# A residual kept by features, or by tokens with a turn at each joint

## The chip, the core and the metric

The kernel runs on one core of a Trainium2 chip. Five engines run their own instruction streams: TensorE (PE) multiplies matrices out of SBUF into PSUM, VectorE (DVE) and ScalarE (ACT) do elementwise work on either memory, GpSimd (POOL) does little here beyond starting DMAs that add into SBUF, and SyncE (SP) starts the other DMAs. The metric is the device time of one execution in microseconds (us).

A matmul has a stationary operand of 128 x 128, loaded into the array before it, and a moving operand that streams past it, here up to 512 columns. In the rows of the profile the moving operand is named first: `ps<-actH,wh` streams `actH` past the stationary `wh`.

## The reference

One layer of a streaming encoder on 512 tokens with 1024 features:

```
h = h + 1/2 * SwiGLU_1(RMSNorm(h))             # 1024 -> 2 x 2816 -> 1024
z = RMSNorm(h) @ W_in                          # conv value, gate, q, k, v, r, low-rank gate
h = h + concat([conv module, gated linear attention]) @ W_out
h = h + 1/2 * SwiGLU_2(RMSNorm(h))
h = h + sigmoid(RMSNorm(h) @ W_g) * (p @ W_p)
out = RMSNorm(h)
```

Everything is float32. A contraction over features needs both operands with features on the partitions; a sum over the features of one token (the RMSNorm) and the output are by tokens.

## The kernel before

**Numbers.** Each float32 operand of a large product is split into two parts that the fast matmul format holds: a high one (a copy on ACT, `act.copy` or `AF.Copy` with a scale) and a low one (source minus high, on DVE). A product is three matmuls: high x high, high x low, low x high (`mm3`, `mul`, `part`). For some weights the subtraction is done by a DMA of POOL that adds into SBUF (`added`): ACT writes the high part and the negated source.

**Layout of the residual.** The residual stream is eight tiles `hT[0..7]` of 128 features x 512 tokens. x arrives by tokens, is turned on PE by 128 x 128 transposes (`turn_x`), and copied into `hT` (`keep_x`, line 461). The down projection of a SwiGLU (`second`, line 745) and the output projection (`part`, line 1228) have the weight as the stationary side, so their PSUM results have features on the partitions and are added to `hT` by DVE. The last stage needs tokens on the partitions, so `inputs` (line 1571) turns pieces of `hT` back, four transposes a call, eight calls.

**RMSNorm.** The gain of the next norm is applied when the high and low parts `hgH`, `hgL` are made. The factor of each token is applied to the results of the product instead, as a row spread over the partitions (`rsb`). `Norm` squares every `hT` tile on ACT, adds the squares on DVE, and sums over partitions with four matmuls against ones (`colsum`).

**Up projections.** Most pairs of column blocks use a scheme of seven products of half-sized blocks (`m1` to `m7`, class `Left` for weight sums, class `Right` for sums of activations). `Right.pieces` makes scaled copies `xg` of `hT` on ACT, and `sums1`, `sums2` add and subtract them on DVE. The last stage (gate with `W_g`) uses the same scheme with tokens as rows (`row_sums`, `row_diff`, `row_last`).

**Down projection.** The 22 blocks of hidden features are cut in five (`CUTS`): four of four blocks, one of six. A cut is four pieces; a piece (`piece`) makes two blocks of 128 output features, from one weight tile of four blocks x 256 columns; each block ends with one DVE add into `hT`. The last cut is done in two halves of three blocks. Pieces stand between the units of the next pair; in the steady state a pair is `m6 m7 m5 m1 m2 piece m4 m3 piece`. Before each unit `drive` issues what later units need: weight loads on SP seven or nine units ahead, the split of a weight four units ahead. Loaded weights, their high and their low parts have six buffers each (`raw`, `wh`, `wl`).

**Order.** From the start to line 1669 the instructions of PE, DVE and ACT each stay in the order in which they are written (`Ordered`). Behind that line the compiler orders them by readiness. PSUM has seven banks for products (`bank`) and one more (`aux`).

**Joints.** Three places take the residual to the next normed product: from the first SwiGLU to `W_in` (line 934), from `W_out` to the second SwiGLU (lines 1356 to 1438), and from the second SwiGLU to the last stage (line 1678). At each, `hgH` of a block is made by ACT directly behind its add, and `hgL` by DVE.

Of the kernel before, what the change touches and what calls it, by code (L numbers as in the profile page):

```python
# [15 lines left out]
P = 128  # L16
# [16 lines left out]
CUTS = ((0, 4), (4, 8), (8, 12), (12, 16), (16, 22))  # L33
# [29 lines left out]
def block_kernel(ctx: ExitStack, tc: tile.TileContext, a: dict, out: bass.AP):  # L63
# [169 lines left out]
    def zblock(w, x, mid={}):  # L233

        ps = bank()
        for k in range(DC):
# [49 lines left out]
    class Norm:  # L286
        def __init__(self, engine=dve):
            self.engine = engine
            self.acc = bt(s="sqacc")
            self.n = 0  # L290

        def add(self, h):
            if self.n == 0:
                act.activation(self.acc, h, AF.Square)
            else:
                sq = tmp("sq", bufs=3)
                act.activation(sq, h, AF.Square)
                self.engine.tensor_tensor(out=self.acc, in0=self.acc, in1=sq, op=ALU.add)
            self.n += 1

        def rows(self):
            return rsqrt_mean(colsum([self.acc]), D, TB)

# [25 lines left out]
    class Right:  # L329
# [3 lines left out]
        def __init__(self, rows, gname):  # L333
            self.rows, self.gname = rows, gname
            self.raw, self.op = {}, {}
            for k in range(2):
                for half in range(2):
                    hs = slice(half * HALF, (half + 1) * HALF)
                    self.op[f"b{k + 1}{half + 1}"] = [tuple(t[:, hs] for t in rows[4 * k + c]) for c in range(4)]

        def pieces(self, k, jp):

            for half in range(2):
                t = self.raw[k, half, jp] = two(bt(s="xg"))
                for jj in range(2):
                    c = 4 * k + 2 * jp + jj
                    act.activation(t[:, jj], hT[c][:, half * HALF:(half + 1) * HALF], AF.Copy, scale=vec(self.gname, c))
# [29 lines left out]
        def steps(self):  # L377

            def go(*todo):
                return lambda *_: [f() for f in todo]  # L380

            return [go(lambda: self.pieces(0, 0)),
                    go(lambda: self.pieces(1, 0), lambda: self.sums1(0)),
                    go(lambda: self.pieces(0, 1), lambda: self.sums2(0)),
                    go(lambda: self.pieces(1, 1), lambda: self.sums1(1)),
                    go(lambda: self.sums2(1))]
# [51 lines left out]
    hT = [big.tile([P, SEQ], F32, tag="H", bufs=DC, name=nm("h")) for _ in range(DC)]  # L438
    hg, xps, xt, squares = [], [], {}, []

    def load_x(c, n):

        nt = TB // n
        for h in range(n):
            tile_ = bt(s="x").rearrange("p (t c) -> p t c", t=nt)
# [14 lines left out]

    def keep_x(c):
        (act.copy if c % 2 else dve.tensor_copy)(hT[c], xps[c])
# [87 lines left out]
    xb = Right(hg, "ffn1_norm")  # L550
    steps = xb.steps()
    steps[0]()
    steps[1]()
# [50 lines left out]
    def ffn(w_in, w_out, x, gname, given, first, rsb, hooks, plain):  # L604


        norm = Norm()
        nhg = []
# [19 lines left out]
        def plus(ps, t, i, name):  # L628
            o = tmp(name)
            dve.tensor_tensor(out=o, in0=ps, in1=t, op=ALU.add)  # L630
            dve.tensor_tensor(out=two(o), in0=two(o), in1=row(i), op=ALU.mult)
            return o
# [31 lines left out]
        def m2(p):  # L664
# [3 lines left out]
            def gate0():  # L668
                p.s0 = silu(plus(p.y, p.a, 0, "g1"))
# [11 lines left out]
        def m5(p):  # L681
            mul(p.x, p.part("s1"), x.op["t1"], False, False)
            p.u = plus(p.w, snap(p.x, "sq", bufs=3), 1, "u1")

        def m4(p):
            mul(p.w, p.part("a22"), x.op["t4"], False, True)
            gated(p, p.s0, plus(p.w, p.u2, 0, "u1"), 0)
# [6 lines left out]
        def plain_unit(j):  # L694

            up, i, k = j // 4, j // 2 % 2, j % 2
            def run(p):
# [15 lines left out]
                return [lambda: gated_block(p, p.s[i], scaled(ps, "u1"), i),  # L713
# [31 lines left out]
        def second(cut):  # L745

            f0, f1 = cut
            last = f1 == CUTS[-1][1]
            kn = f1 - f0
            nk = kn // 2 if last else kn  # L750
            ps = {}

            def piece(n, g, begin, final, key=None):

                def get():
                    got[f0, n, g] = load(w_out, f0 + g * nk, nk, n * P, 2 * P)

                def make():
                    got[f0, n, g] = parts(got[f0, n, g])

                def run():
                    left = []
                    wh, wl = got.pop((f0, n, g))
                    for i in range(2):
                        if begin:
                            ps[n + i] = bank()
                        cs = slice(i * P, (i + 1) * P)
                        for kk in range(nk):
                            k = g * nk + kk
                            f = f0 + k  # L770
                            mm3(ps[n + i], wh[:, kk, cs], wl[:, kk, cs], *pairs[f // 2].acts[f % 2],
                                k == 0, k == kn - 1)
                        if final:
                            h = hT[n + i]
                            dve.scalar_tensor_tensor(out=h, in0=ps[n + i], scalar=0.5, in1=h,
                                                     op0=ALU.mult, op1=ALU.add)
                            if last:
                                hi = bt(F32R, "hgH")
                                act.activation(hi, h, AF.Copy, scale=vec(gname, n + i))
                                left.append((h, hi, vec(gname, n + i)))  # L780
                    if key:
                        hooks.get(key, lambda *_: None)()
                    if not left:
                        return []

                    def lower():
                        for h, hi, g in left:
                            lo = bt(F32R, "hgL")
                            dve.scalar_tensor_tensor(out=lo, in0=h, scalar=g, in1=hi.bitcast(F32),
                                                     op0=ALU.mult, op1=ALU.subtract)  # L790
                            nhg.append((hi, lo))

                    lower()
                    for h, *_ in left:
                        norm.add(h)

                return [(7, get), (AHEAD, make)], run

            if not last:
                return [piece(n, 0, True, True, ("g2", f0) if n == 0 else None) for n in range(0, DC, 2)]  # L800
            return ([piece(n, 0, True, False, ("last", n)) for n in range(0, 6, 2)],
                    [piece(n, 1, False, True, ("rest", n)) for n in range(0, 6, 2)]
                    + [piece(6, 0, True, False, ("rest", 6)), piece(6, 1, False, True, ("rest", 7))])

# [19 lines left out]
        for i in range(start, npair):  # L824
# [3 lines left out]
            if i == end:  # L828
                half, rest = second(cut_of[i])
                units.append(half[0])  # L830
# [10 lines left out]
        units += half[1:] + rest  # L841
# [3 lines left out]
        def first_out(norm_of_rows):  # L845
            got["rsb"] = norm_of_rows
            for i in range(2):
                s = silu(scaled(first[i][0], "g1"))
                gated_block(p0, s, scaled(first[i][1], "u1"), i)
# [7 lines left out]
        return nhg, norm  # L857
# [4 lines left out]
    def sums_hooks(x, names, at):  # L862

        h = {}
        for name, key in zip(names, at):
# [4 lines left out]
    hooks.update({("h%d" % (i + 1), 1): f for i, f in enumerate(steps[2:])})  # L870
    hooks.update({("m5", 3): lambda *_: made[0](), ("m5", 4): lambda *_: constants(),
                  ("m4", 10): lambda *_: w_ahead.append(ahead(w_in, D_CONV, 2 * P)),
                  ("last", 4): lambda *_: w_ahead.append(ahead(w_in, 0, 2 * P))})
    hg, norm = ffn(ffn1_in, a["ffn1_w_out"][0], xb, "mix_norm", {0: Left(ffn1_in, 0), 1: w1},
                   (ps0[:2], ps0[2:]), lambda: spread(mid[0]), hooks, (1, 2))
# [65 lines left out]
    pb0 = zblock(wb[0], hg)  # L941
# [6 lines left out]
    pa0 = zblock(wa[0], hg, {1: lambda: mid.append(rsqrt_mean(colsum([norm.acc]), D, TB))})  # L948
# [267 lines left out]

    def oload(n):
        for i in range(n, n + 2):
            raw_o[i] = load(a["w_out"][0], 0, DC, i * P, P)

    def ohigh(n):
        return (high4 if n in (4, 5) else high)(raw_o[n])
# [5 lines left out]
    def part(ps, w, ks, first, last, mid={}):  # L1228
        for k in ks:
            if k in mid:  # L1230
                mid[k]()
            (wh, wl), (xh, xl) = rows_of(w, k), mix[k]
            pe.matmul(ps, wh, xh, start=(first and k == ks[0]), stop=False)
            pe.matmul(ps, wl, xh, start=False, stop=False)
            pe.matmul(ps, wh, xl, start=False, stop=(last and k == ks[-1]))

    def first_part(n, w, mid={}):
        ps = bank()
        part(ps, w, range(4, 8), True, False, mid)
        half[n] = (w, ps)  # L1240

    oload(0)
    wo, rt = {n: added(ohigh(n)) for n in (0, 1)}, []
    for t in range(TB):
# [20 lines left out]
        if t == 1:  # L1265
            oload(2)
            wo[4] = [added(w) for w in ohigh(4)]
# [7 lines left out]
        if t == 2:  # L1275
            wo[5] = [added(w) for w in ohigh(5)]
# [15 lines left out]
    wo[2] = added(ohigh(2))  # L1292
# [8 lines left out]
    first_part(0, wo[0])  # L1301
    first_part(1, wo[1])
# [6 lines left out]
    low(wo[3])  # L1309
# [476 lines left out]
```

## Time and profile before

| what | value |
|---|---|
| median of 3 runs | 947.41 us (947.36 to 948.08) |
| profiled execution | 947.17 us |
| its span, first to last instruction | 945.5 us |
| mean granted TensorE clock | 0.997 |
| busy PE, DVE, ACT, POOL | 934.8, 747.0, 471.6, 56.4 us |
| HBM read, written | 93.61, 2.10 MB |

Rows of instruction groups give busy time, the mean length of one in ns, and the idle time in front. Nearly all instructions pass through one helper, so every row has line L46; the tile names tell them apart. Matmuls overlap their neighbours: the length of one is more than the distance from one start to the next, and it is the distance that counts on the path.

### The profile page before, as it was taken

The numbers are of one execution on the slowest core, as the hardware profiler recorded it, in microseconds if no ns is written. First come the engines' busy times: TensorE is split into PE (matmuls) and PEld (weight loads), VectorE is DVE, ScalarE is ACT, GpSimd is POOL, SyncE is SP. The second block draws the span as 40 slices with busy tenths as digits, with TensorE's granted clock in tenths as the row PEclk, the third lists the DMA queues.
The fourth block names the chain that finished last, engine by engine and source line by source line (L and its number), as shares of the span: only waits on it lengthen the run. The fifth ranks groups of instructions, "written<-read, shape, count | busy, mean of one in ns | idle before, by whom it ended". The sixth has DMA issues, their size and how long they took to land.

```text
span 945.5 us, 14381 instructions
## 1 busy us (share of the span) xinstructions
PE 934.8 (99%) x5770; PEld 828.2 (88%) x5770; DVE 747.0 (79%) x1021; ACT 471.6 (50%) x713; POOL 56.4 (6%) x71
## 2 busy tenths in 40 slices
PE   9999999999999999999999999999999999999996
PEld 7888999999999988788877889999999999998885
DVE  6786887887788566999986749787878787866896
ACT  5752544334443574463564855444434433445882
POOL 0000200000000110001030010000000000000121
PEclk9999999999999999999999999999999999999998
DMA  7532223242223593346552571432243224347463
GB/s 229 182 123 74 94 79 119 94 134 89 91 89 112 146 254 84 77 109 161 134 132 74 151 178 45 134 110 70 89 134 112 68 91 132 97 149 222 90 111 112
DMA packets 107686, 112.88 MB, mean 119 GB/s; under 512 B 5139, under 2 KB 96453, under 8 KB 107620
## 3 DMA queue, kind: packets, MB, share of 16 engines
q1 hardware_dynamic: 101732, 94.67, 31.9%
q0 software_dynamic: 5872, 17.30, 10.3%
q8 instruction: 45, 0.74, 0.3%
q14 instruction: 21, 0.17, 0.1%
q10 hardware_dynamic: 16, 0.00, 0.0%
HBM read 93.61 MB, written 2.10 MB: 101 GB/s over the span
## 4 chain that ended last, share of the span: by engine, by line
PE 99%; DVE 0%; ACT 0%; POOLq 0%; issue 0%; POOL 0%
PE ps L46 97%; PE ax L46 1%; DVE y L46 0%; POOLq L1782 0%; ACT ycH L46 0%; DVE yc L46 0%; ACT hgH L46 0%; DVE rs L46 0%; ACT s L46 0%; DVE u L46 0%; DVE g L46 0%; DVE s L46 0%; POOL ident masks.py:199 0%; DVE ms L46 0%; POOL mean L46 0%
## 5 line engine op out<-in xcount | busy, mean ns | idle before, releaser
L46 PE MATMUL ps<-hgH,wh 128*128 128x256 f32 (+1 forms) x768 | 238.4, 315 | 0.3 <-ACT hgH L46 0.3
L46 PE MATMUL ps<-hgL,wh 128*128 128x256 f32 (+1 forms) x768 | 237.6, 314 | 0.0
L46 PE MATMUL ps<-hgH,wl 128*128 128x256 f32 (+1 forms) x768 | 237.3, 314 | 0.0
L46 DVE TENSOR_TENSOR wl<-wr,wh 128x1024 fp32r<-128x1024 f32 (+2 forms) x162 | 189.6, 1181 | 47.8 <-ACT wh L46 47.7
L46 ACT CAST wh<-wr 128x1024 fp32r<-128x1024 f32 (+2 forms) x176 | 176.7, 1019 | 30.8 <-PE ps L46 16.3
L46 PEld LDWEIGHTS ps<-hgH,wh 128*128 128x128 f32 x768 | 146.3, 191 | 11.2 <-issue 1.1
L46 PEld LDWEIGHTS ps<-hgL,wh 128*128 128x128 f32 x768 | 146.1, 191 | 9.2 <-issue 0.2
L46 PEld LDWEIGHTS ps<-hgH,wl 128*128 128x128 f32 x768 | 146.4, 191 | 8.8
L46 PE MATMUL ps<-actH,wh 128*128 128x512 f32 x352 | 137.4, 390 | 0.0
L46 PE MATMUL ps<-actL,wh 128*128 128x512 f32 x352 | 137.3, 390 | 0.0
L46 PE MATMUL ps<-actH,wl 128*128 128x512 f32 x352 | 136.9, 389 | 0.0
L46 ACT ACTIVATE s<-g 128x512 f32<-128x512 f32 x48 | 30.4, 633 | 194.3 <-DVE g L46 194.3
L46 DVE SCALAR_TENSOR_TENSOR cv<-glu,cw,cv 128x502 f32<-128x502 f32 (+24 forms) x120 | 81.0, 732 | 0.6
L46 PEld LDWEIGHTS ps<-actH,wl 128*128 128x128 f32 x352 | 66.1, 188 | 14.1
L46 PEld LDWEIGHTS ps<-actH,wh 128*128 128x128 f32 x352 | 66.2, 188 | 12.9
L46 PEld LDWEIGHTS ps<-actL,wh 128*128 128x128 f32 x352 | 66.2, 188 | 12.5
L46 DVE SCALAR_TENSOR_TENSOR h<-ps,h 128x512 f32<-128x512 f32 x80 | 54.1, 687 | 22.2 <-PE ps L46 22.0
L46 ACT COPY sq<-ps 128x512 f32<-128x512 f32 x38 | 22.1, 585 | 73.8 <-PE ps L46 73.8
L46 DVE TENSOR_TENSOR wl<-sm,wh 128x1024 fp32r<-128x1024 f32 x38 | 46.2, 1221 | 1.2 <-ACT wh L46 0.9
L46 ACT CAST actH<-m 128x512 fp32r<-128x512 f32 x44 | 25.5, 618 | 37.3 <-DVE m L46 37.2
L46 ACT CAST wh<-sm 128x1024 fp32r<-128x1024 f32 x38 | 39.5, 1043 | 5.5 <-DVE sm L46 2.9
L46 DVE TENSOR_TENSOR u<-ps,sq 128x512 f32<-128x512 f32 x17 | 11.7, 691 | 34.8 <-ACT sq L46 34.8
(267 smaller groups left out, 1729.5 us busy)
## 6 DMA issues: line engine op xcount, KB each, us to landing
wr<-in_ffn_w_in SPq DMA_DIRECT2D x84, 512.0 KB
wr<-in_ffn_w_out SPq DMA_DIRECT2D x32, 512.0 KB
wr<-in_w_in SPq DMA_DIRECT2D x20, 512.0 KB
wl<-wr POOLq DMA_DIRECT2D x15, 512.0 KB, 5.5
wr<-in_ffn_w_out SPq DMA_DIRECT2D x16, 384.0 KB
wr<-in_w_out SPq DMA_DIRECT2D x8, 512.0 KB
wq<-in_ple_w_gate SPq DMA_DIRECT2D x8, 512.0 KB
wl<-wq POOLq DMA_DIRECT2D x8, 512.0 KB, 5.1
```

The costliest lines, as they stand in the source:

```text
L46: inst = call(*args, **kwargs)
```

## The change

The residual is now one tile `hall` of 128 tokens x 4 x 1024 features, into which x is loaded. The down projection and the output projection have the activations (by 128 tokens) as the stationary side and 512 columns of weight as the moving side; the DVE add that puts the product into `hall` also applies half the norm's factor, which is now one number a partition (`rsh`), so three multiplications by the spread row are dropped from the gating. Squares for the next norm are summed along the row on ACT (`accum_out`), so `colsum` and the DVE adds of squares go. At each joint a new class `Turn` transposes `hall` back to features, eight chunks of four transposes, in two halves of four chunks; ACT and DVE split each chunk out of PSUM, and where the seven-product scheme follows, ACT also writes the two scaled copies (`keep`) that `pieces` wrote before. The transposes of `inputs` go, since the last stage reads `hall`.

The last cut is 20 to 22 now, behind one of 16 to 20. A piece is one half of the output columns and two blocks of tokens; its weight tiles serve two pieces. The tiles of `W_out` are two rows of blocks x 512 columns.

```diff
-CUTS = ((0, 4), (4, 8), (8, 12), (12, 16), (16, 22))
+CUTS = ((0, 4), (4, 8), (8, 12), (12, 16), (16, 20), (20, 22))
...
+        def keep(self, ps, c, by_dve=False):
+            k, jp, jj = c // 4, c % 4 // 2, c % 2
+            for half in range(2):
+                if not jj:
+                    self.raw[k, half, jp] = two(bt(s="xg"))
+                o, src, g = self.raw[k, half, jp][:, jj], ps[:, half * HALF:(half + 1) * HALF], vec(self.gname, c)
+                if by_dve:
+                    dve.tensor_scalar(o, src, g, None, ALU.mult)
+                else:
+                    act.activation(o, src, AF.Copy, scale=g)
...
+    class Turn:
+        def done(self, t, e):
+            act.activation(tmp("sq", bufs=3), h_of(t, e), AF.Square, accum_out=self.ss[:, e * TB + t:e * TB + t + 1])
+
+        def chunk(self, c):
+            ps = bank()
+            for t in range(TB):
+                pe.transpose(ps[:, t * P:(t + 1) * P], hall[:, t, c * P:(c + 1) * P], ident)
+            self.hg.append(gsplit(ps, vec(self.gname, c), "hg"))
+            if self.x is not None:
+                self.x.keep(ps, c)
+
+        def half(self, e):
+            for c in range(4 * e, 4 * e + 4):
+                self.chunk(c)
...
+            def piece(e, th):
                 def get():
+                    for kp in range(0, kn, 2):
+                        got[f0, e, kp] = load(w_out, f0 + kp, 2, e * SEQ, SEQ)
...
+                    for t in (2 * th, 2 * th + 1):
+                        ts, ps = slice(t * P, (t + 1) * P), bank()
+                        for k in range(kn):
...
+                            pe.matmul(ps, xh, wh, start=(k == 0), stop=False)
+                            pe.matmul(ps, xl, wh, start=False, stop=False)
+                            pe.matmul(ps, xh, wl, start=False, stop=(k == kn - 1))
+                        h = h_of(t, e)
+                        dve.scalar_tensor_tensor(out=h, in0=ps, scalar=got["rsh"][:, t:t + 1], in1=h,
+                                                 op0=ALU.mult, op1=ALU.add)
+                        if last:
+                            nxt.done(t, e)
...
+                return [(7, get)] + [(AHEAD - kp // 2, lambda kp=kp: make(kp)) for kp in range(0, kn, 2)], run
+
+            units = [piece(e, th) for e in range(2) for th in range(2)]
+            if last:
+                units.insert(3, ([], lambda: nxt.half(0)))
...
-    pb0 = zblock(wb[0], hg)
+    pb0 = zblock(wb[0], hg, ks=range(4))
+    pa0 = zblock(wa[0], hg, ks=range(4))
+    nxt.half(1)
+    zblock(wb[0], hg, ps=pb0, ks=range(4, DC))
...
+        if n == 5:
+            nxt.half(0)
...
+    g0 = plain_block(w0, 0, 0, ks=range(4))
+    u0 = plain_block(w0, 1, 0, ks=range(4))
+    nxt.half(1)
     steps[0]()
-    g0 = plain_block(w0, 0, 0)
+    plain_block(w0, 0, 0, ps=g0, ks=range(4, DC))
     steps[1]()
+    plain_block(w0, 1, 0, ps=u0, ks=range(4, DC))
...
-        for c in range(4):
-            pe.transpose(pt[:, c * P:(c + 1) * P], hT[4 * e + c][:, ts], ident)
-        return pq, pt
+        return pq, h_of(t, e)
...
     dve.behind(dve.latest, summed)
+    nxt.half(1)
+    a12, a21, a22 = of_rows(1, 0), of_rows(0, 1), of_rows(1, 1)
+    row_sums(0)
     row_sums(1)
```

More of the change, by code (lines that the diff above doesn't have):

```diff
@@ L459, in split_x @@
         hg.append(gsplit(xps[c], vec("ffn1_norm", c), "hg"))
+    xb = Right(hg, "ffn1_norm")
     def keep_x(c):
-        (act.copy if c % 2 else dve.tensor_copy)(hT[c], xps[c])
+        xb.keep(xps[c], c, c % 2 == 0)
     ssx = tmp("ssx", 32, bufs=1)
@@ L781, in run @@
[L781 to L791, printed above, removed]
@@ L840, in ffn @@
                 due += second(cut_of[i])
-        units += half[1:] + rest
+        units += due + second(CUTS[-1])
         p0 = pairs[0]
@@ L856, in ffn @@
         drive(units)
-        return nhg, norm
     w_in = a["w_in"][0]
@@ L1231, in part, with first_part @@
                 mid[k]()
[L1232 to L1240, printed above, removed]
+            (wh, wl), (xh, xl) = o_rows(e, k), mix[k]
+            pe.matmul(ps, xh[:, ts], wh, start=(first and k == ks[0]), stop=False)
+            pe.matmul(ps, xh[:, ts], wl, start=False, stop=False)
+            pe.matmul(ps, xl[:, ts], wh, start=False, stop=(last and k == ks[-1]))
+    def first_part(n, mid={}):
+        half[n] = bank()
+        part(n, range(4, 8), True, False, mid)
     oload(0)
-    wo, rt = {n: added(ohigh(n)) for n in (0, 1)}, []
+    wo, rt = {n: oadded(n) for n in (0, 1)}, []
     for t in range(TB):
```

322 lines of the change are left out of this document (137 added, 185 removed).

## The prediction

> **What bounds the kernel now.** I read the page's busy times first, then the chain that ended last, then windows over the stages that the change touches.
>
> ```profile
> PE 934.8 (99%) x5770; PEld 828.2 (88%) x5770; DVE 747.0 (79%) x1021; ACT 471.6 (50%) x713; POOL 56.4 (6%) x71
> ...
> PE 99%; DVE 0%; ACT 0%; POOLq 0%; issue 0%; POOL 0%
> ```
>
> The busy line alone would not prove it, since matmul records overlap; but the chain runs through PE for 99% of the span. So an instruction added to PE's stream adds its spacing to the time, one removed gives it back, and work of ACT or DVE counts only where PE comes to wait for it.
>
> ```profile
> 231.58:237.05 5.47, 5.47 (x27) 4.51 (x25) 5.31 (x7) 0.71 (x3) 0.00 (x0) 1.00 0.74 227
> 212.00:243.10 31.10, 31.10 (x218) 29.18 (x217) 24.88 (x29) 12.79 (x16) 0.00 (x0) 1.00 0.33 102
> 538.00:545.00 7.00, 7.00 (x33) 5.79 (x32) 6.58 (x11) 7.00 (x15) 0.05 (x1) 1.00 0.42 135
> 882.90:903.70 20.80, 20.80 (x101) 17.30 (x100) 19.53 (x40) 17.97 (x30) 6.79 (x7) 1.00 0.50 95
> ```
>
> The columns are the window, its length, then busy time of PE, weight load, DVE, ACT and POOL, and the granted clock. Row one is one down-projection piece, 24 matmuls of 512 columns (the other three counted are neighbours at its edges): 5.47/24 = 0.228 us each. Row two is one steady pair: DVE 24.9 of 31.1 us, ACT 12.8. Rows three and four are the joint into the second SwiGLU, where ACT is full, and the entry of the last stage, where DVE has 1.3 and ACT 2.8 of 20.8 us free. PE waits in neither today.
>
> **The matmuls that swap sides.** 2 x 528 of the two down projections and 192 of the output projection keep their number and size: 8 x 22 x 3 of 512 columns are 4 x 2 x 22 x 3. The kernel has both kinds of stationary side already (moving operand named first):
>
> ```profile
> L46 PE MATMUL ps<-actH,wh 128*128 128x512 f32 x352 | 137.4, 390 | 0.0
> L46 PE MATMUL ps<-wh,hgH 128*128 128x512 f32 x88 | 34.7, 394 | 0.0
> L46 PE MATMUL ps<-wh,hgL 128*128 128x512 f32 x88 | 34.3, 389 | 0.0
> ```
>
> Streaming weights past activations takes 389 to 394 ns by the same records that give 390 the other way round. I take 0 for the swap.
>
> **The transposes.** Added: 3 joints x 8 chunks x 4 = 96. Removed: 8 calls of `inputs` x 4 = 32, and three column sums.
>
> ```profile
> 485.38 1.47 PE L46 MATMUL ps<-ident,y 128*128 128x128 f32 x12
> 486.69 1.02 PE L46 MATMUL ax<-cv,mean 128*128 128x512 f32 x2
> ...
> 896.10 0.60 PE L46 MATMUL ps<-ident,h 128*128 128x128 f32 x4
> 896.46 0.48 PE L46 MATMUL ps<-wh,pTH 128*128 128x512 f32 x1
> 896.77 0.40 PE L46 MATMUL ps<-wh,pTL 128*128 128x512 f32 x1
> ...
> 363.63 0.95 PE L46 MATMUL ax<-ones,sqacc 128*128 128x1 f32 x8
> 364.44 0.49 PE L46 MATMUL ps<-hgH,wa 128*128 128x512 f32 x1
> 364.76 0.40 PE L46 MATMUL ps<-hgL,wa 128*128 128x512 f32 x1
> ```
>
> Start to start, twelve take 486.69 - 485.38 = 1.31 us, 0.109 each. A call's four take 0.36, and the first matmul behind them 0.31 in place of 0.228, together 0.44. A column sum takes 0.81, and 0.09 more behind it, 0.90. So 96 x 0.109 + 6 half-joints x 0.08 = 11.0 us come in, 8 x 0.44 + 3 x 0.90 = 6.2 go: **+4.8 us on the path**. Nothing hides this, as PE has no free time.
>
> [...]
>
> **The joint into the second SwiGLU.** Before, `hgH` of a block followed its add and the copies `xg` came later. Now both wait for a transposed chunk, in ACT's order.
>
> ```profile
> 536.56 0.73 ACT L46 ACTIVATE hgH<-h,vcol 128x512 fp32r<-128x512 f32 x1 [1.57 <-DVE h L46]
> 537.19 0.62 ACT L46 ACTIVATE sq<-h 128x512 f32<-128x512 f32 x1
> 537.71 4.89 ACT L46 ACTIVATE xg<-h,vcol 128x256 f32<-128x256 f32 x12
> 542.51 1.03 ACT L46 CAST wh<-wr 128x1024 fp32r<-128x1024 f32 x1
> 543.45 1.06 ACT L46 ACTIVATE wl<-wr 128x1024 fp32r<-128x1024 f32 x1
> ...
> L46 DVE SCALAR_TENSOR_TENSOR hgL<-ps,vcol,hgH 128x512 fp32r<-128x512 f32 x8 | 5.7, 747 | 3.9 <-ACT hgH L46 3.9
> L46 DVE SCALAR_TENSOR_TENSOR h<-ps,h 128x512 f32<-128x512 f32 x80 | 54.1, 687 | 22.2 <-PE ps L46 22.0
> ```
>
> By starts, a high part is 0.63 us of ACT, a copy (542.51 - 537.71)/12 = 0.40; a chunk is 0.63 + 2 x 0.40 = 1.43. PE needs a chunk every 3 x 0.228 = 0.68 us behind `half(1)`. That half's last add (n = 7) is covered by 24 matmuls, 5.5 us, against 0.69 for the add, and `half(0)` by three products. Counted from the first transpose of `half(1)`: chunk 4 is there at 0.45, its high part at about 1.15, chunk 7's at 1.15 + 3 x 1.43 = 5.45, its low part 0.75 later, 6.2. PE ends the transposes at 1.75 and reaches chunk 7's low part at 1.75 + 3 x 0.68 + 0.23 = 4.0. **It waits 2.2 us.** The floor is 0, if ACT gets both halves done earlier; the ceiling is ACT's whole half, 5.7.
>
> **The joint into the last stage.** Between the end of piece `d20,0` and the first product of the last stage PE has three pieces of 12 matmuls and 16 transposes, 3 x 2.73 + 1.75 = 9.9 us. Squares with a row sum, which exist in the last stage, start 0.62 apart:
>
> ```profile
> 907.07 0.63 ACT L46 ACTIVATE u<-cv 128x512 f32<-128x512 f32 x1
> 907.60 0.19 ACT L46 ACTIVATION_READ_ACCUMULATOR u<-cv 128x1 f32 x1
> 907.69 0.62 ACT L46 ACTIVATE u<-cv 128x512 f32<-128x512 f32 x1
> ```
>
> ACT has six of these queued, and in the hooks two `q_high` and two `third_sum`, six instructions of 0.95 like the cast at 542.51: 9.4 us before chunk 0. So chunk 0's high part begins as PE arrives, PE waits for it and its low part, some 1.2 us, then takes 6 x 0.228 = 1.37 a chunk against ACT's 1.43: **1.4 us**. DVE's adds of piece `d20,3` stand behind the four low parts of `half(0)`, but their readers, the transposes of `half(1)`, come only behind this product. `half(1)` then costs **0.4** in the same way as above, PE again taking 1.37 a chunk. Behind it ACT is late. The stage has lost two high parts, two squares, four copies of `row_sums` and two short casts of the difference there, and gained most of `half(0)`, two squares and `half(1)`: 5.1 + 1.2 + 5.7 - (1.3 + 1.0 + 1.6 + 0.6) = 7.5 us net, and row four of the windows has 2.8 free. What comes next late is `b3`: ACT's two instructions, then the DMA of POOL.
>
> ```profile
> wl<-wq POOLq DMA_DIRECT2D x8, 512.0 KB, 5.1
> ```
>
> I put its landing at 24 us behind the last down projection, PE at 22.7: **1.5 us**, in all 3.3. Floor 0 (the compiler orders this region by readiness, and can move the two casts of `project` into ACT's gaps), ceiling 5 (all of ACT's added work exposed: 16 copies x 0.40, less the four copies and two short casts, 2.2, and about 1 for the first chunk).
>
> **The joint into `W_in`** has no copies: ACT 0.63 and DVE about 0.6 a chunk beat PE's 0.68. PE's two half products, 5.5 us, cover the last add. The `rsqrt` chain has 15 matmuls, 3.4 us, before it is spread, where it had 24, and DVE has one subtraction of a weight in front of it:
>
> ```profile
> L46 DVE TENSOR_TENSOR wl<-wr,wh 128x1024 fp32r<-128x1024 f32 x142 | 171.8, 1221 | 35.7 <-ACT wh L46 35.7
> ```
>
> I put **0.3**, between 0 and that subtraction's 1.2.
>
> **Loads, queues, buffers.** SP issues two weight tiles for a half of the columns at once, seven units ahead; bytes are the same. Each serves two pieces, with `m4` and `m3` between, so high tiles live longer: at the start of `m4` six are live (`a22`, `s4`, two of the piece, `s2`, `s1`), and the cast of `s3` must wait for the end of `m4`, 24 matmuls of 256, 2.9 us. Behind it on ACT and DVE stand the subtraction and `m4`'s add. `s3` is used four units later, and DVE has 6.2 us a pair free and loses two row multiplications:
>
> ```profile
> L46 DVE TENSOR_TENSOR u<-u,bc 128x512 f32<-128x512 f32 x34 | 23.5, 692 | 1.2
> ```
>
> I take 0. The eight extra DVE adds a SwiGLU (0.69 each) lie in the same room. `W_out`'s tiles are as many, the accumulating DMAs too. The start keeps its order; `keep` costs ACT 0.3 us more a chunk for four chunks and removes `pieces` later. The tail behind PE's last matmul keeps its instructions.
>
> **The sum**, against the profiled execution's 947.17 us (span 945.5 and 1.7 around it; 0.24 under the median): 947.2 + 4.8 + 2.2 + 3.3 + 0.3 = 957.8. All floors give 952.0, all ceilings 947.2 + 4.8 + 5.7 + 5 + 1.2 = 963.9.
>
> **The rivals.** No change that a measurement here could tell is 0.2%, 1.9 us.
> *The joints are hidden.* ACT reaches each chunk in time, and only PE's own 4.8 us remain, 952. For it: ACT is half idle over the span. Against: rows three and four, the two joints where it isn't.
> *Weight buffers.* If `s3`'s wait takes DVE's room, PE loses in each of 17 pairs. At 1 us a pair this is +17 on the floor, 969. It decides once waits in a pair pass 6.2 + 1.4 us. Against: one wait of 2.9.
> *Slow transposes.* At the start the same instruction is spaced wider:
>
> ```profile
> 1.61 2.40 PE L46 MATMUL ax<-ident 128*128 128x128 f32 x10 [1.61 <-POOL ident masks.py:199]
> 4.07 0.27 PE L46 MATMUL ax<-ident,vcol1r 8*128 8x8 f32 x1
> ```
>
> 2.46/10 = 0.246. If blocks of 16 brought this back, 96 x 0.137 = 13 us come on top of the forecast, 971. Against: the twelve at 485.38 came every 0.109, and the granted clock of their window, the last column but two, is 1.00:
>
> ```profile
> 484.80:488.50 3.70, 3.70 (x24) 2.69 (x22) 1.35 (x2) 1.32 (x3) 1.23 (x2) 1.00 1.07 251
> ```
>
> [...]
> *Faster.* The 1,248 swapped matmuls would have to start closer together with the activations stationary. At 8 ns each, 10 us, it balances my sum; at 12 ns the time is 957.8 - 15 = 942.8. Against: 390 and 389 to 394 ns.
>
> **How the numbers follow.** Forecast (954 to 961) 0.50; joints hidden (951 to 954) 0.20; weight buffers 0.10; slow transposes 0.05; faster 0.04; within 0.2%, when the joints are hidden and the transposes are cheaper still, 0.04; anything else slower 0.07. The range 951 to 964 takes in the first two, the ceilings and part of the last, 0.8. Slower: 0.92.
>
> **What would show it.** Right: 96 transposes out of `hall` about 0.109 apart; PE's idle time before `hgH` and `hgL` matmuls behind `half(1)` of the second joint, put down to ACT or DVE, about 2 us; a share of ACT or DVE in the chain of some 5 us around the joints; a steady pair still 31.1 us. Wrong: a pair longer than 31.1 us, or a piece other than 5.47 us, or ACT with gaps at the joints.

## The result, and the profile after

The changed kernel takes 970.50 us (median of 4 runs, 968.50 to 972.22), the kernel before 947.75 us (947.36 to 949.59) beside it. The ratio is 1.0235, with a 95% interval of 1.0208 to 1.0263: 2.35% slower. The direction was forecast; the size, 957.8 us in a range of 951 to 964, was not: the change costs twice what the sum gave.

The page of the changed kernel, busy times and the chain that ended last:

```profile
PE 948.2 (98%) x5810; PEld 833.0 (86%) x5810; DVE 722.5 (75%) x967; ACT 476.5 (49%) x733; POOL 56.2 (6%) x71
...
PE 93%; ACT 3%; DVE 2%; issue 0%; DMA 0%; POOL 0%; POOLq 0%; SPq 0%; ACTq 0%; DVEq 0%
```

PE's share of the chain fell from 99% to 93%, and ACT and DVE hold 5% of it, 48 us, where the prediction had named some 5 us. The windows say where they are. The span is cut at the same work in both kernels: at the spread of the first norm's root, at that of the second, at the spread inside the output projection, at that of the third norm, at the second turn of `p`, at the first product of `n2`, at PE's last start. First the kernel before; columns as in the prediction (window, length, busy time of PE, weight load, DVE, ACT, POOL, granted clock, DMA):

```profile
0.00:34.09 34.09, 32.16 (x156) 26.70 (x156) 22.31 (x37) 22.40 (x38) 2.79 (x10) 1.00 0.75 237
34.09:370.02 335.93, 335.93 (x2121) 305.54 (x2120) 259.07 (x316) 151.96 (x210) 13.53 (x16) 1.00 0.39 114
370.02:508.58 138.56, 138.56 (x858) 110.46 (x857) 128.08 (x213) 74.42 (x148) 18.37 (x21) 1.00 0.49 120
508.58:552.23 43.65, 43.42 (x197) 35.48 (x196) 28.09 (x44) 29.90 (x46) 4.54 (x5) 1.00 0.47 110
552.23:844.04 291.81, 291.81 (x1980) 271.67 (x1979) 232.64 (x270) 127.79 (x168) 1.78 (x2) 1.00 0.35 107
844.04:897.93 53.89, 53.89 (x270) 45.79 (x269) 38.95 (x57) 37.19 (x54) 5.51 (x7) 1.00 0.59 154
897.93:936.66 38.73, 38.73 (x197) 32.51 (x195) 33.35 (x72) 26.86 (x48) 8.93 (x10) 1.00 0.53 109
936.66:945.50 8.84, 0.28 (x3) 0.07 (x1) 4.51 (x15) 1.09 (x2) 0.92 (x1) 0.73 0.31 119
```

And the changed kernel, cut at the same work:

```profile
0.00:34.30 34.30, 32.09 (x155) 26.68 (x156) 22.89 (x41) 20.18 (x34) 2.78 (x10) 1.00 0.75 236
34.30:373.16 338.86, 338.84 (x2145) 308.01 (x2144) 248.52 (x295) 150.12 (x208) 13.50 (x16) 1.00 0.38 112
373.16:511.74 138.58, 138.58 (x858) 110.44 (x857) 128.50 (x215) 74.36 (x148) 18.34 (x21) 1.00 0.49 123
511.74:564.56 52.82, 50.62 (x220) 39.34 (x219) 26.07 (x42) 32.45 (x58) 4.59 (x5) 0.94 0.37 89
564.56:856.37 291.81, 291.81 (x1980) 271.65 (x1979) 220.49 (x246) 128.21 (x164) 1.72 (x2) 1.00 0.35 110
856.37:919.69 63.32, 59.87 (x290) 47.05 (x288) 39.95 (x54) 43.95 (x74) 7.27 (x9) 1.00 0.53 130
919.69:956.56 36.87, 36.10 (x168) 29.73 (x168) 30.69 (x59) 25.76 (x44) 6.48 (x7) 1.00 0.47 100
956.56:967.50 10.94, 0.28 (x3) 0.07 (x1) 5.38 (x19) 1.51 (x4) 1.51 (x2) 0.71 0.25 97
```

Subtracting row by row: +0.2 at the start, +2.9 with the joint into `W_in`, 0, **+9.2 with the joint into the second SwiGLU**, 0 in the steady pairs, **+9.4 up to the first product of `n2`**, -1.9 from there to PE's last start, +2.1 behind it; together 22.0, the whole difference of the spans. The reader is to see two things. All of it lies at the joints and the end, none in the steady work between them: rows three and five, 430 us, are the same within 0.02, and in row two the 320.71 us up to the first transpose have their counterpart, 320.71 us for as many matmuls, in the kernel before. And in the fourth row the granted clock is 0.94.

Row four close up, in the timeline of the changed kernel behind the transposes of `half(1)` (start, length, what, and in brackets the idle time before it and what ended it):

```profile
546.69 0.69 ACT L46 ACTIVATE hgH<-ps,vcol 128x512 fp32r<-128x512 f32 x1 [4.13 <-PE ps L46]
547.41 0.75 DVE L46 SCALAR_TENSOR_TENSOR hgL<-ps,vcol,hgH 128x512 fp32r<-128x512 f32 x1 [5.75 <-ACT hgH L46]
...
548.20 0.84 ACT L46 ACTIVATE xg<-ps,vcol 128x256 f32<-128x256 f32 x2 [0.82 <-DVE hgL L46]
...
548.93 0.69 ACT L46 ACTIVATE hgH<-ps,vcol 128x512 fp32r<-128x512 f32 x1
549.65 0.75 DVE L46 SCALAR_TENSOR_TENSOR hgL<-ps,vcol,hgH 128x512 fp32r<-128x512 f32 x1 [1.48 <-ACT hgH L46]
```

A chunk goes ACT, DVE, ACT, one after the other: high part, low part, the two copies, then the next chunk's high part, 548.93 - 546.69 = 2.24 us a chunk, where the prediction had 1.43. That ACT stands still while DVE makes the low part is in ACT's list of waits too (500 to 570 us; us in total, times, longest):

```profile
ACT xg L46 <- DVE hgL L46: 6.6, 8, 0.8
```

The copies read the PSUM bank that the low part reads too, and they wait for it, 0.82 us each time, at all eight chunks of this joint. That one reader waits for the other is what the trace shows; why it does, no run shows. The prediction had not weighed this.

### The profile page after: what moved, and what is told of

Its sections match the earlier page's. It is cut to its first block, busy times and chain, and to the rows that moved or that the text cites. A ratio compares the mean times of both kernels' runs of the same rounds, so it can differ in the third digit from the quotient of the medians.

```text
span 967.5 us, 14435 instructions
## 1 busy us (share of the span) xinstructions
PE 948.2 (98%) x5810; PEld 833.0 (86%) x5810; DVE 722.5 (75%) x967; ACT 476.5 (49%) x733; POOL 56.2 (6%) x71
## 4 chain that ended last, share of the span: by engine, by line
PE 93%; ACT 3%; DVE 2%; issue 0%; DMA 0%; POOL 0%; POOLq 0%; SPq 0%; ACTq 0%; DVEq 0%
PE ps L46 92%; ACT xg L46 1%; PE ax L46 1%; ACT hgH L46 1%; ACT wh L46 1%; ACT sq L46 1%; DMA wr<-in_ffn_w_in 0%; DVE hgL L46 0%; DVE g L46 0%; DVE s L46 0%; ACT wl L46 0%; DVE rs L46 0%; DVE y L46 0%; DVE sq L46 0%; DVE xg L46 0%
## 5 line engine op out<-in xcount | busy, mean ns | idle before, releaser
L46 DVE TENSOR_TENSOR wl<-wr,wh 128x1024 fp32r<-128x1024 f32 (+1 forms) x158 | 188.6, 1208 | 61.0 <-ACT wh L46 60.8
L46 ACT CAST wh<-wr 128x1024 fp32r<-128x1024 f32 (+1 forms) x172 | 176.3, 1039 | 74.3 <-PE ps L46 41.4
L46 PE MATMUL ps<-wh,actH 128*128 128x512 f32 x352 | 137.6, 391 | 0.0
L46 PE MATMUL ps<-wh,actL 128*128 128x512 f32 x352 | 137.3, 390 | 0.0
L46 PE MATMUL ps<-wl,actH 128*128 128x512 f32 x352 | 137.0, 389 | 0.0
L46 DVE SCALAR_TENSOR_TENSOR hall<-ps,rsh,hall 128x512 f32<-128x512 f32 x96 | 71.1, 747 | 30.1 <-PE ps L46 29.2
L46 PEld LDWEIGHTS ps<-wl,actH 128*128 128x128 f32 x352 | 66.1, 188 | 13.9
L46 PEld LDWEIGHTS ps<-wh,actH 128*128 128x128 f32 x352 | 66.2, 188 | 12.9
L46 PEld LDWEIGHTS ps<-wh,actL 128*128 128x128 f32 x352 | 66.2, 188 | 12.4
L46 DVE SCALAR_TENSOR_TENSOR hgL<-ps,vcol,hgH 128x512 fp32r<-128x512 f32 x32 | 23.2, 748 | 30.9 <-ACT hgH L46 30.7
```

The source lines that it names most:

```text
L46: inst = call(*args, **kwargs)
```

## The experiments

**The order of the readers (e1, e2).** Both leave the computation as it is. e1 issues the copies ahead of the low part:

```diff
-            self.hg.append(gsplit(ps, vec(self.gname, c), "hg"))
+            hi, lo, g = bt(F32R, "hgH"), bt(F32R, "hgL"), vec(self.gname, c)
+            act.activation(hi, ps, AF.Copy, scale=g)
             if self.x is not None:
                 self.x.keep(ps, c)
+            dve.scalar_tensor_tensor(out=lo, in0=ps, scalar=g, in1=hi.bitcast(F32), op0=ALU.mult, op1=ALU.subtract)
+            self.hg.append((hi, lo))
```

> In each chunk of the joints the two copies of ACT are issued ahead of DVE's low part; nothing else changes. Theory (the copies wait 0.82 us each time for the low part, which reads the same bank; pace of a chunk 2.23 us): the pace falls to about 1.4 us, ACT's waits for hgL (8.2 us, 10 times) go, and the joint into the second SwiGLU falls from 50.75 us to about 46.5 (some 3 us of the 6.4 us of waits, and the 1.4 us of the slow matmuls behind them); the last stage falls from 110.96 by 2 to 4 us, so 963 to 966 in all against 970.5. DVE's low parts then come 0.8 us later in each chunk. Rival (ACT's and DVE's amount of work sets the pace, the order does not matter): within 1 us of 970.5, with the joint still at 50 or more.

e2 gives the copies of the second joint to DVE:

```diff
-                self.x.keep(ps, c)
+                self.x.keep(ps, c, self.gname == "ffn2_norm")
```

> At the joint into the second SwiGLU alone DVE makes the copies in place of ACT. Theory (one reader of a bank after the other, but ACT's high part of the next chunk is no longer behind the copies): pace of a chunk is DVE's work, 0.75 + 2 x about 0.3 = 1.35 us, the joint 46 to 47 us in place of 50.75, the whole 966 to 967; the last stage unchanged at 111 us. Rival (the amount of work on both engines together, or the transposes themselves, set the joint): the joint stays above 50 us.

e1 takes 962.28 us (962.06 to 962.81; ratio to before 1.0156, 1.0141 to 1.0171), e2 965.44 (1.0191, 1.0174 to 1.0208); both are a little below the range expected. The same work, in another order, is 8.2 us shorter. To compare the joints, one window in each kernel: from the first transpose of `half(1)` over these 16 transposes and the 168 matmuls of 512 columns (and one spread) behind them. The changed kernel:

```profile
546.05:592.91 46.86, 44.90 (x190) 35.02 (x188) 28.33 (x42) 25.48 (x39) 4.53 (x5) 0.93 0.42 101
```

e1:

```profile
546.51:589.76 43.25, 41.47 (x190) 33.44 (x189) 28.33 (x42) 25.05 (x39) 4.48 (x5) 1.00 0.46 110
```

e2:

```profile
546.60:589.50 42.90, 41.47 (x189) 33.44 (x188) 31.19 (x50) 22.13 (x31) 4.53 (x5) 1.00 0.47 111
```

3.6 and 4.0 us shorter, with DVE's busy time unchanged in e1 and ACT's nearly so. The joint isn't all that e1 gained: between the two profiled executions (spans of 967.5 and 960.6 us) another 2.1 us lie at the entry of the last stage and 1.7 behind the first product of `n2` (both below), and 0.5 was lost at the start. In e1 the wait has changed sides, as DVE's list over 500 to 570 us shows:

```profile
DVE hgL L46 <- ACT xg L46: 12.1, 8, 6.6
```

Now the low part waits for the copies, and ACT runs through: the trace has its high parts at 547.15, 548.45, 549.73 and 551.01, 1.29 us a chunk. The amount of work was not what set 2.24; the order of two readers of a bank was. That it is the shared bank, and not something else that copies and low part have in common, was not shown: it is the author's reading, and a second bank for the copies wasn't tried, since the kernel has no four banks of PSUM free there.

**More work between the transposes and their first use (e4).**

```diff
     nxt.half(1)
+    g1_ = plain_block(w0, 0, 1, ks=range(4))
+    u1_ = plain_block(w0, 1, 1, ks=range(4))
```

(the second halves of both follow behind those of `g0` and `u0`; the root and its spread are hung into them)

> At the joint into the second SwiGLU the first halves (k 0 to 3) of the other two products of w0 are issued between the transposes of half 1 and their first use: 24 matmuls of 0.228 us, 5.5 us of work that needs only half 0. Theory (PE waits there for the chunks, 6.4 us, of which the clock's fall behind the gaps is a consequence): the waits of half 1 almost go, the clock stays at 1.00, the joint falls from 50.75 us to 44 to 46 us, the whole to 964 to 966. Rival (the time is PE's own, transposes or clock): the joint stays within 1 us of 50.75.

962.87 us (961.54 to 963.95; 1.0161, 1.0146 to 1.0176), 7.6 less than the changed kernel, and again below the range expected. The window of the joint in e4:

```profile
545.87:586.17 40.30, 40.30 (x189) 33.67 (x188) 28.07 (x42) 25.60 (x39) 4.54 (x5) 1.00 0.49 118
```

46.86 - 40.30 = 6.56 us: PE is busy throughout and the clock is 1.00. So the joint cost 9.2 us, of which 6.4 to 6.6 were PE's waits and their consequences, and 2.75 PE's own work (32 x 0.109 + 2 x 0.08 - 0.90). e1's order left 43.25 - 40.30 = 2.95 of it.

**The clock (e10, e11).** Behind the waits the changed kernel's matmuls start 427 ns apart: the timeline has seven of them from 555.52 to 558.08. Windows over the waits and behind them give the granted clock (last but two):

```profile
547.72:551.90 4.18, 2.44 (x9) 0.95 (x7) 1.21 (x3) 2.83 (x6) 0.00 (x0) 0.95 0.01 2
551.90:555.52 3.62, 3.39 (x6) 1.58 (x6) 2.10 (x4) 2.03 (x5) 0.00 (x0) 0.50 0.00 0
555.52:558.08 2.56, 2.56 (x8) 1.98 (x6) 2.30 (x5) 2.56 (x4) 0.00 (x1) 0.50 0.00 0
```

After some 4 us in which PE was busy for 2.44 the clock is halved, for about 6 us. That the waits are the reason, and not what ACT and DVE do meanwhile, is tried by putting useless work into them: e10 fills the waits with matmuls, e11 with transposes, into a bank that nothing reads:

```diff
+    def fill():
+        idle = aux()
+        for _ in range(4):
+            pe.matmul(idle, w0.part("a11")[0][:, 0, 0:P], hg[0][0], start=True, stop=True)
-    plain_block(w0, 0, 0, ps=g0, ks=range(4, DC))
+    plain_block(w0, 0, 0, {k: fill for k in range(4, DC)}, g0, range(4, DC))
...
+        for _ in range(8):
+            pe.transpose(idle[:, 0:P], ident, ident)
```

> The changed kernel, and in the waits of the joint into the second SwiGLU, ahead of the products with chunks 4 to 7, four matmuls of 512 columns into a bank that nothing reads (0.91 us each time, in gaps of 1.55 us a chunk). Theory (the chunks' pace of 2.23 us sets this place; the clock fell because PE stood idle for most of 9 us, and the seven matmuls of 427 ns behind it come from that): the filling costs nothing, the clock stays at 1.00, the matmuls behind the waits come every 228 ns, and the 168 matmuls from the first transpose of half 1 on take 45 to 46 us in place of 46.86; whole 969 to 970. Rival (the slow matmuls come from contention with ACT or DVE, not from idle time): they stay at 427 ns, the stretch at 46.9 or more.

> As e10, with eight transposes of the identity (0.87 us) in place of the four matmuls. If transposes keep the clock up as matmuls do, as e10: 45 to 46 us. [...]

967.54 us (967.02 to 968.36) and 968.00 us (966.79 to 968.33): with useless work added, both are shorter than the changed kernel, by 3.0 and 2.5 us. The window of the joint in e10:

```profile
545.84:591.11 45.27, 44.70 (x206) 36.47 (x204) 28.33 (x42) 25.48 (x39) 4.53 (x5) 1.00 0.44 105
```

and in e11:

```profile
545.81:591.09 45.28, 44.71 (x221) 37.10 (x220) 28.33 (x42) 25.47 (x39) 4.53 (x5) 1.00 0.43 105
```

ACT and DVE are as busy as in the changed kernel, PE stands idle for 0.6 us in place of 2.0, and the clock stays up. So PE's idle time had brought it down, and 46.86 - 45.27 = 1.59 us of the joint were the clock's. The medians fell by more, 3.0 and 2.5 us. The runs of the changed kernel give a hint: two, of 968.50 and 969.31 us, have a mean clock of 0.993, the other two, of 971.69 and 972.22 us, have 0.991, so these lost more to the clock than the profiled execution (969.31 us) shows. e10's profiled execution, the longest of its four, has a second fall, in the last stage, behind PE's wait for the sums of `n2`:

```profile
919.71:923.36 3.65, 3.65 (x11) 2.86 (x9) 3.65 (x9) 3.24 (x5) 1.76 (x2) 0.53 0.94 136
```

The profiled execution of the changed kernel keeps its clock at the same place:

```profile
921.50:925.15 3.65, 3.65 (x17) 2.99 (x16) 3.65 (x9) 3.27 (x5) 1.79 (x2) 1.00 0.90 136
```

That its two longer runs fell there is likely, but not shown, since they have no trace. In e11 the clock stayed at 1.00 through the joint with these fp32 transposes in the waits, as in e10 with matmuls. In the changed kernel no single wait of PE at this joint was longer than 0.72 us, and a part-idle stretch, 2.44 busy us of 4.18, was enough for the fall to 0.50.

**The end (e3).** The last four calls of `inputs` get their four transposes again, into a bank that nothing reads.

```diff
+        if back:
+            pt = bank()
+            for c in range(4):
+                pe.transpose(pt[:, c * P:(c + 1) * P], hall[:, t, (4 * e + c) * P:(4 * e + c + 1) * P], ident)
```

> The last four calls of inputs (2,0), (3,0), (0,1), (1,1) get four transposes of hall each again, into a bank that nothing reads; their other operands are as in the changed kernel. Theory (the end is bound by ACT's and DVE's chain from w_ on, PE is ahead there): within 0.5 us of the changed kernel, 970.5, so the 1.8 us that the prediction credited for these calls were not on the path. Rival (PE sets the end): 1.75 us more, 972.3.

971.36 us (969.12 to 971.99), 0.9 above the changed kernel and inside its runs; the medians alone don't decide. The windows do: from the first product of `n2` to PE's last start, and behind it, in e3:

```profile
919.59:958.08 38.49, 37.73 (x183) 31.38 (x184) 31.76 (x64) 26.30 (x45) 7.43 (x8) 1.00 0.45 96
958.08:967.30 9.22, 0.28 (x3) 0.08 (x1) 4.52 (x15) 1.09 (x2) 0.92 (x1) 0.66 0.30 115
```

PE ends 38.49 - 36.87 = 1.6 us later, and what follows it is 10.94 - 9.22 = 1.7 us shorter. The end doesn't move. The chain of the changed kernel says why: at 947.00, some 20 us before the end, it leaves PE for DVE and the engines behind it, where that of before stayed on PE up to 936.95, 9 us before the end:

```profile
939.86 7.04 PE ps L46 x31
...
947.00 0.70 DVE s L46
...
947.72 0.59 DVE g L46
```

**The entry of the last stage (e5, e6).** Here the chain of the changed kernel is on ACT from 888.64 on:

```profile
888.82 0.94 ACT wh L46
...
892.89 0.67 ACT wh L46
...
894.78 0.95 ACT wq L46
895.73 1.23 ACT sq L46 x4
896.96 0.57 ACT hgH L46
```

Chunk 0's high part starts at 896.86; PE had its transposes done at 894.22. Ahead of it stand the hooks of `d20,0` and `d20,1`, and ahead of those, at the first square of `d20,0`, ACT had been idle for 5.8 us:

```profile
886.73 0.63 ACT L46 ACTIVATE sq<-hall 128x512 f32<-128x512 f32 x1 [5.81 <-DVE hall L46]
```

e5 is e1 with these hooks one unit earlier:

```diff
-                  ("d16", 3): todo((q_high, b11, q11, 1)),
-                  ("d20", 0): todo((q_high, b21, q21, 0), (first_sum, 0), (third_sum, 0)),
-                  ("d20", 1): todo((q_high, b21, q21, 1), (first_sum, 1), (third_sum, 1)),
+                  ("d16", 3): todo((q_high, b11, q11, 1), (q_high, b21, q21, 0), (first_sum, 0), (third_sum, 0)),
+                  ("d20", 0): todo((q_high, b21, q21, 1), (first_sum, 1), (third_sum, 1)),
```

> As e1 (copies ahead of the low part), and in the last pieces of the second SwiGLU the two q_high, first_sum, third_sum pairs of hooks stand one unit earlier (d16,3 and d20,0 in place of d20,0 and d20,1). In e1 ACT is idle 5.8 us ahead of the squares of d20,0 and then busy without a break into chunk 0, whose high part starts 2.6 us after its transposes. Theory (the order in ACT's queue makes the entry into the last stage late, not the amount of its work): from the first transpose of that joint to the first product of n2 25.05 us in e1 become 22.5 to 23.5, the whole 960 to 961.2 against 962.3. Rival (ACT's whole work up to n2, or the DMA of b3, sets it): within 0.6 us of e1.

e6 is e1 with the copies of the last joint on DVE, behind its low part:

```diff
+            last = self.gname == "ple_norm"
-            if self.x is not None:
+            if self.x is not None and not last:
                 self.x.keep(ps, c)
...
+            if last:
+                self.x.keep(ps, c, True)
```

> As e1 at the joint into the second SwiGLU; at the joint into the last stage DVE makes the sixteen copies, behind its low part. Theory (ACT is the engine that is late in the last stage, it has a queue without a gap from chunk 0 to n2): ACT loses 16 x 0.37 = 5.9 us there, DVE, with some 6 us of gaps in that stretch, takes them; the stretch to n2 falls from 25.05 us to 23 to 24, the whole to 960.5 to 961.5. Rival (DVE becomes the late one, or the waits are the DMA's): 962 or more.

e5 takes 960.69 us (959.40 to 961.82; 1.0129, 1.0111 to 1.0148), 1.6 less than e1; e6 965.07 (1.0177, 1.0160 to 1.0193), 2.8 more. The window from the first transpose of this joint to the first product of `n2`, in the changed kernel:

```profile
892.55:919.69 27.14, 23.69 (x105) 16.12 (x103) 18.30 (x27) 25.45 (x49) 4.11 (x6) 1.00 0.50 95
```

in e1:

```profile
889.40:914.45 25.05, 22.04 (x106) 16.55 (x104) 18.16 (x27) 23.51 (x48) 2.90 (x4) 1.00 0.44 82
```

in e5:

```profile
890.75:913.88 23.13, 21.72 (x106) 16.51 (x104) 17.93 (x27) 21.15 (x46) 1.50 (x2) 1.00 0.24 46
```

in e6:

```profile
889.67:916.91 27.24, 23.21 (x106) 16.03 (x104) 23.64 (x43) 19.67 (x33) 7.03 (x8) 1.00 0.58 109
```

e1 to e5 is 1.9 us: the hooks belong into ACT's idle time. In e6 ACT is down to 19.7 busy us and DVE up to 23.6 of 27.2: the lateness only moved to DVE, where each chunk's copies now stand ahead of the next low part and, at the end, ahead of the sums for `n2`. My theory for e6, that DVE's gaps would take them, fell; its rival held.

**All together (e7, e8).** e7 is e1 with e4. e8 adds e5's hooks, and lets DVE put the last piece, `d20,3`, into `hall` before the low parts of chunks 2 and 3 (the squares of that piece follow behind the chunks on ACT):

```diff
+                def early():
+                    turned.extend(nxt.turned(c) for c in range(4))
+                    for c in range(2):
+                        nxt.drain(c, turned[c])
+
+                def late():
+                    for c in range(2, 4):
+                        nxt.drain(c, turned[c])
+                    for te in behind:
+                        nxt.done(*te)
+
+                units.insert(3, ([], early))
+                units.append(([], late))
```

> e1 and e4 together. Theory (two places: the waits behind half 1 of the second joint, gone with e4; the last stage, 3.7 us shorter with e1): the effects add outside the second joint, 970.5 - 6.6 - 3.7 = 960.2, with 959 to 961 as the bounds; the joint as in e4, 38.6 us for its 168 matmuls. Rival (what e1 gave in the last stage was chance of the order there): 962 to 964, as e4 alone.

> e7, the hooks as in e5, and DVE's two adds of the piece d20,3 ahead of the low parts of chunks 2 and 3 (with their squares behind the chunks on ACT). Theory: the waits of the last stage's entry fall from 5.1 us in e1 to 1 to 3; whole 956 to 958.5. What then stays above the 947.6 of before is PE's own work, 4.8 us by the rows, 0.3 at the joint into W_in, and the end that no longer follows PE. Rival (the work itself costs more than 0.109 us a transpose, or a steady pair is longer): still above 960.

959.20 us (1.0121, 1.0101 to 1.0140) and 956.98 us (955.97 to 957.29; 1.0089, 1.0074 to 1.0104). Both as expected. e7's entry of the last stage takes 25.06 us, e1's was 25.05, so that gain was not chance. In e8 it is

```profile
888.05:909.39 21.34, 20.98 (x106) 16.50 (x104) 17.28 (x26) 21.09 (x45) 1.44 (x2) 1.00 0.27 50
```

and the joint into the second SwiGLU 40.30 us as in e4. 27.14 - 21.34 = 5.8 and 6.56 come back, 12.4 of the changed kernel's 22 us, by order alone. (The medians differ by 13.5, the profiled executions by 11.9.) No version here beats the kernel before.

**The price of a transpose (e9).** e8 with each transpose of the joints twice, into the same place:

```diff
-            for t in range(TB):
+            for t in 2 * list(range(TB)):
```

> e8 with every transpose of the three joints issued twice into the same place: 96 more on PE, nothing else changed. Theory (a transpose is 0.109 us of PE's path where PE does not wait): the joints into W_in and into the second SwiGLU take 64 x 0.109 = 7.0 us more, the one into the last stage up to 3.5 more, less what its waits of e8 (about 1.5 us) swallow; whole 957.0 + 9 to 10.5 = 966 to 967.5. Rival (transposes come out cheaper, hidden in part beside weight loads or waits): under 963. Rival (slow transposes, 0.246 us, or a fall of the clock): 975 or more.

967.41 us (966.99 to 968.09; 1.0212, 1.0195 to 1.0229): 10.4 us for 96 transposes, 0.109 each on average. The joint into the second SwiGLU, from the first transpose of `half(0)` to the spread, in e8:

```profile
532.73:564.82 32.09, 32.09 (x160) 27.06 (x158) 14.37 (x26) 21.19 (x39) 5.34 (x6) 1.00 0.51 108
```

and in e9:

```profile
533.58:569.16 35.58, 35.58 (x191) 30.56 (x190) 14.32 (x26) 21.19 (x39) 5.36 (x6) 1.00 0.51 104
```

35.58 - 32.09 = 3.49 = 32 x 0.109, with PE busy throughout in both. The other places are less clean, so the average of the whole is a fit in part by luck: the joint into `W_in` grew by 3.1 us (18.18 to 21.31), 0.098 a transpose; the entry of the last stage grew by 5.3 (21.34 to 26.62), where at most 3.5 were expected, since PE stands idle there for an estimated 2.1 us (26.62 less e8's 20.98 of work and 32 x 0.109) in place of 0.4; and e9's profiled execution had come to the joint into `W_in` 2.3 us sooner (354.81 against 357.10), with the same code up to there (see the end). Slow transposes, 975 us or more, are out.

## Why the prediction was right, and where it failed

**The transposes, 0.109 us each: right.** e9 measured it directly at the joint into the second SwiGLU, 3.49 us for 32, and the clock stayed at 1.00.

**Swapped sides 0, weight buffers 0, the pairs: right.** In the changed kernel the swapped matmuls have the same length as before, 391 ns against 390:

```profile
L46 PE MATMUL ps<-wh,actH 128*128 128x512 f32 x352 | 137.6, 391 | 0.0
```

The wait that was predicted for the weight buffers came, as ACT's list of waits over the whole span shows: its casts of a weight wait for PE 18 times more often (it was 16.3 us, 5 times, before):

```profile
ACT wh L46 <- PE ps L46: 47.1, 23, 12.5
```

It costs nothing, as predicted: the fifth rows of the windows are 291.81 us in both.

**The joint into `W_in`, +0.3 beside its work: right.** 2.9 us in all, of which 32 x 0.109 + 0.16 - 0.90 = 2.75 are work and 0.2 is left.

**The joint into the second SwiGLU, 2.2 us of waits: wrong, 6.4.** The step that failed is "a chunk is 0.63 + 2 x 0.40 = 1.43". It added ACT's own work and left out that the copies stand behind DVE's low part of the same bank; 2.24 was measured. With the order of e1 the pace was 1.29 and the waits 2.95 us, near the 2.2 of the sum. The stated ceiling, ACT's whole half of 5.7 us, was too low too, since it held neither the 0.82 us of standing still a chunk nor the clock's 1.6. No engine's work was mis-sized; a wait between two engines was missing, and it brought a second loss, the clock, with it.

**The last stage, 3.3 us of waits: wrong, about 7.1.** The stretch up to `n2` grew by 9.4, of which 2 x (16 x 0.109 + 0.08) - 0.90 - 0.44 = 2.3 are work (only one call of `inputs` has its transposes in that stretch in the kernel before). The step "chunk 0's high part begins as PE arrives" failed: it began 2.6 us after the transposes, because the hooks' 6 us on ACT came behind 5.8 us of idling instead of in it; e5 gave 1.9 back for it. The `b3` step named the wrong culprit. Its sum is also off by a little, since 24 less 22.7 is 1.3 and not 1.5, and the 24 has no working. PE did wait ahead of `n2` for about as long, but for the sums, which come out of the late chunks over DVE and ACT, not for POOL's DMA, so the near agreement is luck. PE's list of waits from 885 to 921 us in the changed kernel has:

```profile
PE ps L46 <- ACT sH L46: 1.6, 1, 1.6
```

In e1, e5 and e8, whose chunks are earlier, that wait is gone, and 0.3 us for a sum on DVE is left. e8, which at this joint mends only the order of ACT and DVE, has 21.34 us from the first transpose to `n2`, where the changed kernel had 27.14, against 32 x 0.109 + 0.16 + 72 x 0.228 = 20.1 of work.

**The credit for `inputs`, 8 x 0.44 = 3.5: wrong for seven of the eight calls.** In the kernel before, the transposes of seven calls lie behind the first product of `n2`. PE did finish that part 1.9 us sooner, and the work behind PE grew by 2.1 (rows seven and eight of the windows). The prediction said "the tail behind PE's last matmul keeps its instructions": so it does, but it is not PE that they wait for. e3 put 16 of these 28 transposes back and the end stayed where it was. From the first product of `n2` to the end of the span the kernel before takes 47.6 us, the changed kernel 47.8; so none of the 3.1 us came. In e1, e5, e7 and e8 it is 46.1 to 46.2, and in e4, whose chunks are as late as the changed kernel's, 46.9: part of the credit comes with another order, and which step frees it stays open.

**The sum.** Work on the path 4.8 + 3.1 for the lost credit, 0.2 at `W_in`, waits 6.4 and 7.1, 0.2 at the start: 21.8 of the 22.0 us. The forecast's parts were 4.8, 0.3, 2.2 and 3.3. The rival "joints hidden" was the wrong side of the truth; that both joints could be late by two to three times the estimate was in no rival. That the changed kernel mended in four places ends at 957.0, near the 957.8 forecast, is partly coincidence: it still has waits in the last stage, and a tail that does not follow PE.

## What to carry to other kernels

When two engines drain the same PSUM bank, look whether one waits for the other (here 0.82 us at each of eight chunks); if so, count them one after the other, not side by side, and try the other order: the order alone was worth 8.2 us here (e1). When an instruction leaves PE's stream, look behind it for the engine that sets the end before crediting it. Where PE must wait, other work that is ready can pay twice, since a part-idle PE here also lost its clock (0.50 for some 6 us, 1.59 us of the joint).

## What was not expected of the hardware

The granted clock fell to 0.50 for some 6 us though no single wait of PE ahead of it was longer than 0.72 us; PE had been busy 2.44 of 4.18 us. In e1, with waits of up to 0.75 us and PE busy 3.93 of the 5.71 us behind the transposes, it did not fall. What decides between the two was not tried; the longest single wait does not tell them apart. Nor does the code: ahead of and behind the first product of `n2` PE waits 1.6 and 0.8 us in the changed kernel, and the clock behind reads 1.00 there and 0.53 in e10's profiled execution, where the code is the same.

The runs of one kernel scatter by 0.8 to 3.7 us, and part of it is seen at the start: the first eight matmuls of 512 columns took 1.9 us in one profiled execution and 3.5 in another, whose code up to there is the same. The windows from 6.4 to 10 us of the changed kernel:

```profile
6.40:10.00 3.60, 3.59 (x17) 2.84 (x18) 2.25 (x4) 1.31 (x2) 0.00 (x0) 1.00 1.04 342
```

and of e8:

```profile
6.40:10.00 3.60, 3.57 (x9) 2.72 (x10) 1.96 (x3) 0.62 (x1) 0.00 (x0) 1.00 1.04 338
```

Nine starts of matmuls in place of seventeen, at a granted clock that reads 1.00 in both. What sets the two apart no run shows. For a difference of 1 us between two kernels the windows are the better measure.
